# The projection behind the attention in pairs of column groups, three of its eight pairs of K tiles by seven products

## The chip, the cores and the metric

The kernel runs on one core of a Trainium2 chip. The metric is device time in microseconds (us) of the whole program, the median of several executions. Within the core TensorE (PE) multiplies, VectorE (DVE) and ScalarE (ACT) prepare operands and evict results, SyncE (SP) and GpSimd (POOL) issue the transfers from memory. Each engine works through its own queue in order; semaphores release an instruction that waits for another engine.

## The reference

One layer of a streaming encoder on 256 tokens (T) of width 2048 (D), float32 throughout. The parts that the change touches are the output projection of the cross attention and the start of the second feed-forward:

```python
x = x + 0.5 * swiglu(rms_norm(x, ffn1_norm[l]), ffn1_w_up[l], ffn1_w_down[l])
...                                   # in-projections, HGRN2, RG-LRU, gated merge
x = x + merged @ w_out[l]
x = x + cross_attention(rms_norm(x, xattn_norm[l]), rms_norm(mem, mem_norm[l]),
                        xattn_wq[l], xattn_wkv[l], xattn_wo[l])
x = x + 0.5 * swiglu(rms_norm(x, ffn2_norm[l]), ffn2_w_up[l], ffn2_w_down[l])
return rms_norm(x, final_norm)

def swiglu(h, w_up, w_down):          # D_FF = 5632
    gate, up = jnp.split(h @ w_up, 2, axis=-1)
    return (jax.nn.silu(gate) * up) @ w_down

def cross_attention(h, m, wq, wkv, wo):   # 4 heads of 512, 256 memory tokens
    ...
    o = jnp.einsum('bhsm,bmhd->bshd', p, v).reshape(B, S, D)
    return o @ wo
```

## The kernel before

**Split operands.** Every float32 operand is held as two parts: a high part `h` (ACT's copy into the matmul type, L153) and a low part `l` (DVE's difference between the value and `h`, L154). A product is three matmuls: high by high, low by high and high by low. `xh`, `xl` are the parts of activations, `h`, `l` those of weights; `h` and `l` come from pools of three buffers each, and a weight buffer `raw` of 1 MB from a pool of three (in the second feed-forward two more, `raw2`, in memory that earlier stages use for other tiles). PSUM has eight banks (`acc`).

**Pairs of K tiles.** In the feed-forwards and in the projection `out` behind the gated merge, two K tiles are multiplied with two groups of columns at a time. A *mixed* (plain) pair does this by eight products, 24 matmuls. A *fast* pair does it by seven products, 21 matmuls, in the manner of Strassen and Winograd: it needs sums and differences of the operands (`xs`, a difference for part of them `xd`; L601) and three differences of the weights (`td`, L334, L336, L338), which are split too (their high part by ACT, their low part `tl` by DVE, both as two pieces of 1024 columns). In an *added* pair (M) the low part of the weights costs DVE nothing: ACT writes the negative copy and an accumulating transfer issued by POOL adds the float32 weights to it. Of the first four groups of the second feed-forward 25 fast pairs are *ready*: their `td` was worked out during the middle of the program, went to memory as a tensor `t`, and is loaded (1024 KB) beside the rest of the weights (768 KB).

**Stages.** Projections of the memory to keys and values; first feed-forward; the in-projections, the two recurrences and their merge; `out`; the projection for q, beside which the heads of the attention run as generators that are advanced a step at a time (`pump`); `o`, the projection behind the attention; the second feed-forward in eleven groups of eight pairs; the final norm. `out` takes its products from a table of pairs, `"m0 f1 M2 f3 m4 f5 M6 m7"`, once for each two column groups (`pair_products`), and `add_residual` adds a finished pair of column groups to the residual stream: six operations of DVE and a copy of ACT once the early banks are done, five at the end.

**`o` before.** It multiplies by `rows_product` (L388): 16 blocks of four K tiles by 512 columns, 24 matmuls each (L393, L394, L399), in the order of `OUT_ORDER`. For each block the weights of 1 MB are split whole (`h` by ACT, `l` 128x2048 by DVE). A finished column group c is added to the residual by `to_residual` (two operations, L1297), and `to_ffn(c)` makes operands of the second feed-forward from it: eight transposes by TensorE (L550), scaled copies, `xh`, `xl`, then eight sums of 128x128 (L601) and their parts. For c = 0 to 2 this stands in `o`, for c = 3 it comes in two halves within the first pairs of the feed-forward.

**The second feed-forward before.** Its first group (`ffn_order`) has fast pairs 0 to 5, all ready, and mixed pairs 6 and 7; in the second group pairs come as 1, 3, 4, 0, 2, 5, 6, 7. Weights are asked for up to two pairs ahead. The order within each engine's queue comes from the tile framework's scheduler, in which loads may move far ahead of the place where the code names them.

## Time and profile before

| | |
|---|---|
| median of 3 runs | 2406.14 us (2405.97 to 2406.42) |
| profiled execution | 2406.76 us |
| its span, first to last instruction | 2405.0 us |
| granted TensorE clock | 0.999 |
| PE, DVE, ACT busy | 2393.3, 2054.2, 1560.6 us |
| transfers | 640 MB, 266 GB/s mean |

A row of the chain of waits gives start, length, engine, tile, line and how many instructions were joined; a row of the windows gives the stretch, its length, and busy time and instructions of PE, PEld (weight loads), DVE, ACT, POOL, then the granted clock, the DMA share and GB/s; a row of a timeline gives start, length, engine, line, operation, what is written from what, shapes and count, and in brackets how long the engine was idle before and what ended it. The projection `o` ends at 1721.93 us; `out` runs from 1430 to 1516.

### The profile page before, as it was taken

To read this page: it belongs to the slowest core of one execution; us is meant where nothing else is said; L and a number is where in the kernel's file an instruction comes from. 1 tells how busy PE (TensorE), PEld (TensorE's weight loads), DVE (VectorE), ACT (ScalarE), POOL (GpSimd) and SP (SyncE) were. 2 spreads that over 40 slices of the span, in tenths; PEclk is the share of its full clock that TensorE was granted. 3 is DMA by queue.
4 is the path that set the end of the run, shared out by engine and by line. 5 is a ranking of instruction groups with operands and counts; after the bars stand their busy time and mean duration, and the time that the engine had idled before them with its cause. 6 is when DMAs were issued, how large, how long until landed. Compare 5 with 4: busy or idle time off the path is not lost.

```text
span 2405.0 us, 31008 instructions
## 1 busy us (share of the span) xinstructions
PE 2393.3 (100%) x12053; PEld 1991.5 (83%) x12053; DVE 2054.2 (85%) x2335; ACT 1560.6 (65%) x1594; POOL 120.1 (5%) x174
## 2 busy tenths in 40 slices
PE   9999999999999999999999999999999999999998
PEld 7888888888888888888888888888888888888887
DVE  7679999999999866778678788765799999999995
ACT  6756777777777654454576456655676677777774
POOL 0000000000000000000000000000000000000000
PEclk9999999999999999999999999999999999999999
DMA  8876889999999757767678768764687899999993
GB/s 301 309 254 223 268 266 266 273 274 278 276 276 276 266 216 291 265 243 289 258 276 334 281 243 262 294 223 162 215 321 299 317 276 276 274 274 273 274 272 129
DMA packets 98739, 640.03 MB, mean 266 GB/s; under 512 B 10976, under 2 KB 11488, under 8 KB 32928
## 3 DMA queue, kind: packets, MB, share of 16 engines
q1 hardware_dynamic: 74160, 493.61, 54.8%
q0 software_dynamic: 24288, 144.19, 24.5%
q8 instruction: 94, 1.54, 0.2%
q14 instruction: 53, 0.43, 0.0%
q10 hardware_dynamic: 144, 0.26, 0.0%
HBM read 601.18 MB, written 36.83 MB: 265 GB/s over the span
## 4 chain that ended last, share of the span: by engine, by line
PE 97%; DVE 2%; DMA 1%; ACT 0%; issue 0%; SPq 0%; ACTq 0%; DVEq 0%
PE acc L698 38%; PE acc L700 19%; PE acc L367 11%; PE acc L393 7%; PE acc L394 7%; PE acc L399 7%; PE acc L370 6%; PE acc L738 1%; PE acc L550 1%; DVE tl L154 1%; DVE l L154 0%; PE acc L1342 0%; PE acc L1088 0%; DMA raw<-t 0%; PE acc L1367 0%
## 5 line engine op out<-in xcount | busy, mean ns | idle before, releaser
L153 ACT ACTIVATE h<-raw 128x2048 fp32r<-128x2048 f32 (+3 forms) x420 | 683.2, 1640 | 412.6 <-PE acc L394 135.0
L154 DVE TENSOR_TENSOR l<-raw,h 128x2048 fp32r<-128x2048 f32 (+2 forms) x365 | 751.6, 2060 | 227.4 <-ACT h L153 224.9
L698 PE MATMUL acc<-h,xh 128*128 128x512 f32 x1221 | 474.6, 391 | 0.6 <-ACT h L153 0.5
L698 PE MATMUL acc<-h,xl 128*128 128x512 f32 x1221 | 473.1, 390 | 0.0
L153 ACT ACTIVATE h<-td 128x1024 fp32r<-128x1024 f32 x287 | 301.0, 1055 | 172.3 <-DVE td L334 53.7
L154 DVE TENSOR_TENSOR tl<-td,h 128x1024 fp32r<-128x1024 f32 x287 | 348.9, 1220 | 13.7 <-ACT h L153 11.8
L698 PE MATMUL acc<-h,hidop 128*128 128x512 f32 x1408 | 351.4, 391 | 0.0
L698 PEld LDWEIGHTS acc<-h,hidop 128*128 128x128 f32 x1408 | 262.7, 188 | 53.8
L698 PEld LDWEIGHTS acc<-h,xh 128*128 128x128 f32 x1221 | 229.1, 188 | 54.6 <-ACT h L153 5.8
L698 PEld LDWEIGHTS acc<-h,xl 128*128 128x128 f32 x1221 | 229.3, 188 | 46.7
L393 PE MATMUL acc<-h,ops 128*128 128x512 f32 x576 | 226.1, 393 | 0.0
L394 PE MATMUL acc<-h,ops 128*128 128x512 f32 x576 | 224.4, 390 | 0.0
L367 PE MATMUL acc<-ops,h 128*128 128x512 f32 x896 | 217.7, 393 | 0.0
L700 PE MATMUL acc<-tl,xh 128*128 128x512 f32 x660 | 193.0, 394 | 0.3 <-DVE tl L154 0.3
L367 PEld LDWEIGHTS acc<-ops,h 128*128 128x128 f32 x896 | 164.1, 188 | 32.6
L700 PE MATMUL acc<-l,hidop 128*128 128x512 f32 x704 | 190.7, 389 | 0.0
L334 DVE TENSOR_TENSOR td<-raw 128x1024 f32<-128x1024 f32 x146 | 178.0, 1219 | 3.5 <-DMA raw<-wout 2.3
L700 PE MATMUL acc<-l,xh 128*128 128x512 f32 x561 | 156.7, 390 | 0.0
L700 PEld LDWEIGHTS acc<-l,hidop 128*128 128x128 f32 x704 | 132.1, 188 | 27.8
L700 PEld LDWEIGHTS acc<-tl,xh 128*128 128x128 f32 x660 | 120.7, 188 | 33.8 <-DVE tl L154 10.1
L399 PE MATMUL acc<-l,ops 128*128 128x512 f32 x576 | 142.3, 389 | 0.0
L399 PEld LDWEIGHTS acc<-l,ops 128*128 128x128 f32 x576 | 108.1, 188 | 22.4
(270 smaller groups left out, 3014.4 us busy)
## 6 DMA issues: line engine op xcount, KB each, us to landing
raw<-wu SPq DMA_DIRECT2D x151, 1024.0 KB, 6.9
raw<-wd SPq DMA_DIRECT2D x88, 1024.0 KB, 7.3
l<-wu POOLq DMA_DIRECT2D x59, 768.0 KB, 8.7
raw<-win SPq DMA_DIRECT2D x40, 1024.0 KB, 4.9
raw<-wg SPq DMA_DIRECT2D x32, 1024.0 KB, 5.4
prep<-wu POOLq DMA_DIRECT2D x25, 1024.0 KB, 7.1
t<-prep POOLq DMA_DIRECT2D x25, 1024.0 KB, 4.6
raw<-t SPq DMA_DIRECT2D x25, 1024.0 KB, 6.5
```

The source lines that it names most:

```text
L153: done["high"] = act.activation(h, raw, ACT.Copy).ins
L154: done["low"] = dve.tensor_tensor(out=l, in0=raw, in1=h.bitcast(F32), op=ALU.subtract).ins
L334: dve.tensor_tensor(out=two[0], in0=raw[:, None, :512].broadcast_to([P, 2, 512]), in1=two[1], op=ALU.subtract)
L367: pe.matmul(acc, h[:, k * P:(k + 1) * P], xs[k], start=k == 0, stop=False)
L370: done["product"] = pe.matmul(acc[:, :T], l[:, k * P:(k + 1) * P], xs[k][:, :T], start=False, stop=k == KT - 1).ins
L393: pe.matmul(accs[t], x[:, t * P:][:, :P], h[j], start=first and j == 0, stop=False)
L394: pe.matmul(accs[t], x[:, T + t * P:][:, :P], h[j], start=False, stop=False)
L399: done["product"] = pe.matmul(accs[t], x[:, t * P:][:, :P], l[j], start=False, stop=last and j == 3).ins
L550: pe.transpose(acc[:, z * T + t * P:][:, :P], tile[:, t * 512 + (2 * y + z) * P:][:, :P], ident)
L698: pe.matmul(acc, a, b, start=start, stop=False)
L700: done["product"] = pe.matmul(acc, ah, bl, start=False, stop=stop).ins
L738: pe.transpose(acc[:, z * T + t * P:][:, :P], hid[t][:, (2 * y + z) * P:][:, :P], ident)
```

## The change

`o` is computed like `out`: by `pair_products` with the same table, in two rounds of two column groups, each with eight pairs of K tiles, three of them by seven products (f1, f3, f5), two added (M2, M6), three plain. The weights `wo` are laid out for pairs. The heads write their results into operands for pairs, with the sums that fast pairs need. `add_residual` takes the place of `to_residual`. The operands of the second feed-forward come in halves of four transposes for every c: those of c = 0 and 1 behind pairs 1, 3, 5 and 6 of the second round of `o`, those of c = 2 and 3 within the first pairs of the feed-forward. The first group of the feed-forward now has mixed pairs 0 and 7 and fast pairs 1 to 6, pair 0 added; still 25 pairs are ready. The heads are advanced by four steps instead of two within the projection for q, and have more, smaller steps.

```diff
@@ -22,9 +22,6 @@
 HEADS = 4
 HD = D // HEADS
 LEVELS = [1, 2, 4, 8, 16, 32, 64]
-
-OUT_ORDER = [(g, kq) for g in range(2) for kq in range(3)] + [(0, 3), (1, 3)]
-OUT_ORDER += [(g, kq) for g in (2, 3) for kq in range(4)]
 BACC = {"dynamic_dma_scratch_size": 1024}
@@ -47,7 +44,7 @@
 KINDS = {"m": "mixed", "M": "mixed", "f": "fast", "a": "fast"}
-PAIRED = {"out": "m0 f1 M2 f3 m4 f5 M6 m7"}
+PAIRED = {"out": "m0 f1 M2 f3 m4 f5 M6 m7", "o": "m0 f1 M2 f3 m4 f5 M6 m7"}
 def kinds(name):
@@ -65,7 +62,7 @@
-    out = [("mixed" if p > 5 else "fast", 0, p) for p in range(8)] if every else first(0)
+    out = [("fast" if 0 < p < 7 else "mixed", 0, p) for p in range(8)] if every else first(0)
     down = [("down", 0, 1, c, 0) for c in range(4)]
     for g in range(1, NG):
         if every:
@@ -165,6 +162,8 @@
             src = wd[e[4], e[3]] if e[0] == "down" else wu[e[1], e[2]]
             kind = "fast" if e[0] == "fast" else "plain"
             if name == "ffn1" and e[0] == "mixed" and f"M{e[2]}" in FIRST[e[1]]:
+                kind = "added"
+            if name == "ffn2" and e == ("mixed", 0, 0):
                 kind = "added"
             if e[0] == "down" and e[4] < NG - 1 and e[4] % 2 == 0 and e[3] % 2 and (e[4] or name == "ffn1"):
                 kind = "added"
@@ -209,8 +208,7 @@
             plan_rows(name, w, g)
     plan_pairs("out", wout)
     plan_columns("q", wq, range(KT))
-    for g, kq in OUT_ORDER:
-        plan.append((("o", g, kq), wo[g, kq], "plain"))
+    plan_pairs("o", wo)
     first_second = len(plan)
     plan_ffn("ffn2", wu2, wd2)
@@ -579,8 +577,8 @@
             h, l = slot(F32R, "xh"), slot(F32R, "xl")
             split(h[:, :512], l[:, :512], g)
             less = None
-            if every and q == 3:
-                if not i:
+            if every and 2 * q + i in (0, 7):
+                if not q:
                     xd.append(slot(F32R, "xd"))
                 less = [xd[-1][:, a:a + 256] for a in (512 * i, 512 * i + 256)]
             if not every and 2 * q + i in BOTH:
@@ -1291,10 +1289,6 @@
             merge(g // 2, accs)
             accs = []
-    def to_residual(c, accs):
-        for t in range(2):
-            o = xt[c][:, t * 512:(t + 1) * 512]
-            dve.tensor_tensor(out=o, in0=accs[t], in1=o, op=ALU.add)
     while under_way:
         next(under_way.pop(0)[1])
     parts.close()
@@ -1317,8 +1311,9 @@
     while under_way:
         next(under_way.pop(0)[1])
     parts.close()
-    parts.enter_context(scope(prep=2, kt=2))
+    parts.enter_context(scope(wide=3, kt=2))
     qs, os = Operands(), Operands()
+    pairs_o = Pairs("o", os)
     rmem = scoped["norms"].tile([P, T], F32, name="rmem", tag="rstd")
     nc.gpsimd.dma_start(rmem, kept_r)
@@ -1366,10 +1361,12 @@
                 s, p = vs[t], ps[:, t * 512:(t + 1) * 512]
                 pe.matmul(acc, s[:, j * P:(j + 1) * P], p, start=(t == 0), stop=False)
                 pe.matmul(acc[:, :T], s[:, 512 + j * P:512 + (j + 1) * P], p[:, :T], start=False, stop=(t == 1))
-            os.add(summed(acc))
-            if j == 1:
-                yield
-        yield True
+            if j % 2 == 0:
+                x = pairs_o.room()
+            os.add(summed(acc, out=x[:, j % 2 * T:][:, :T]))
+            if j % 2:
+                pairs_o.add()
+            yield j == 3
     for m in range(KT):
         if m % 4 == 2:
@@ -1382,43 +1379,40 @@
         qs.add(summed(acc))
         if m % 4 == 3:
             side.append(head_at)
-        pump(2)
+        pump(4)
     pairs2, sums2, sq4 = [], [], TokenSquares()
     def gain2(k):
         return col("ffn2_norm", k)
-    def to_ffn(c):
-        out = []
-        sums2.append(operand_pairs(turned(xt[c]), gain2, c, slot(name="xg"), out, every=True))
-        pairs2.extend(out)
-        if c < 2:
-            sums2.pop(0)()
-
-    out3 = []
-
-    def to_ffn_half(y):
+    halves = {}
+
+    def to_ffn(c, y):
         if not y:
-            out3.append(slot(name="xg"))
-            out3.append([])
-        sums = operand_pairs(turned(xt[3], [y]), gain2, 3, *out3, every=True)
-        pairs2.append(out3[1][-1])
-        if y:
+            halves[c] = slot(name="xg"), []
+        sums = operand_pairs(turned(xt[c], [y]), gain2, c, *halves[c], every=True)
+        pairs2.append(halves[c][1][-1])
+        if y and c < 2:
+            sums()
+        elif y and c == 2:
+            sums2.append(sums)
+        elif y:
             sums2.extend(lambda n=n: sums(((0, n), (1, n))) for n in ("less", "sums"))
-    accs = {}
-    for c, kq in OUT_ORDER:
-        if kq == 0:
-            accs[c] = [bank(), bank()]
-        while len(os.tiles) < 4 * kq + 4:
+    def before_o(g, p):
+        while len(os.tiles) < 2 * p + 2:
             pump(2)
-        rows_product(accs[c], os.tiles, weights("o", c, kq), 4 * kq, kq == 0, kq == 3)
-        flush(late)
+
+    def behind_o(g, p):
         pump(2)
-        if kq == 3:
-            to_residual(c, accs[c])
+        if g and p in (1, 3, 5, 6):
+            flush(late, 1)
+
+    for g in range(2):
+        pair_products("o", g, pairs_o, add_residual, behind_o, before_o)
+        for c in (2 * g, 2 * g + 1):
             sq4.add(c)
-            late += [lambda c=c: to_ffn(c)] if c < 3 else [lambda y=y: to_ffn_half(y) for y in range(2)]
+            late += [lambda c=c, y=y: to_ffn(c, y) for y in range(2)]
     middle.close()
     assert not made_ahead and not under_way
@@ -1553,7 +1547,7 @@
         "wu1": up(a["ffn1_w_up"][0]), "wd1": down(a["ffn1_w_down"][0]),
         "win": win, "wv": rows(w[:, 2048:3072]), "wg": wg, "wab": wab, "wout": pairs(a["w_out"][0]),
         "wq": columns(a["xattn_wq"][0]), "wk": columns(wkv[:, :D]), "wvm": in_quarters(rows(wkv[:, D:])),
-        "wo": rows(a["xattn_wo"][0]),
+        "wo": pairs(a["xattn_wo"][0]),
         "wu2": up(a["ffn2_w_up"][0]), "wd2": down(a["ffn2_w_down"][0]),
     }
```

Line numbers after the change are two or three lower than before (L154 is L151, L698 is L696, L700 is L698, L601 is L599).

On DVE, around the end of `o` (the residual additions of column group 3 and what follows them), before; `l` and `tl` are low parts of weights, `xl` of activations, `x3_94` a residual tile, the numbers behind the names those of buffers in order of their allocation:

```order
L154 TENSOR_TENSOR tl_14126<-raw_14119,h_14125 128x1024 x2
L1297 TENSOR_TENSOR x3_94<-acc_14002,x3_94 128x512
L1297 TENSOR_TENSOR x3_94<-acc_14003,x3_94 128x512
L154 TENSOR_TENSOR l_14181<-raw_14176,h_14180 128x1536
L520 TENSOR_REDUCE stdt_14445<-sst_13472 128x2
L154 TENSOR_TENSOR tl_14185<-raw2_14178,h_14184 128x1024 x2
L154 TENSOR_TENSOR l_14249<-raw2_14244,h_14248 128x1536
```

and with the change, from the first of the five final additions of the second round (`x2_93` and `x3_94`):

```order
L686 TENSOR_TENSOR x2_93<-acc_13889,x2_93 128x512
L151 TENSOR_TENSOR xl_14136<-xs_14185,xh_14135 128x512
L151 TENSOR_TENSOR xl_14182<-xs_14185,xh_14181 128x512
L686 TENSOR_TENSOR x2_93<-acc_13890,x2_93 128x512
L686 TENSOR_TENSOR x3_94<-acc_13892,x3_94 128x512
L686 TENSOR_TENSOR x3_94<-acc_13891,x3_94 128x512 x2
L151 TENSOR_TENSOR l_14311<-raw2_14306,h_14310 128x1536
L151 TENSOR_TENSOR tl_14261<-raw2_14254,h_14260 128x1024 x2
```

Five additions and two low parts of c = 1's sums stand where two additions stood, and the next low part is that of the third pair (`l_14311`, `raw2`), ahead of the second pair's `tl_14261`.

On DVE, towards the end of the feed-forward's first group, before (`l_14419` and `l_14455` are the mixed pairs 6 and 7, `xs_14369` the sums of c = 3):

```order
L154 TENSOR_TENSOR l_14387<-raw_14382,h_14386 128x1536
L154 TENSOR_TENSOR xl_14240<-xs_14369,xh_14239 128x512
L601 TENSOR_TENSOR xs_14369<-xg_14231,xs_14369 128x128
L154 TENSOR_TENSOR tl_14391<-raw_14384,h_14390 128x1024 x2
L154 TENSOR_TENSOR xl_14287<-xs_14369,xh_14286 128x512
L154 TENSOR_TENSOR l_14419<-raw_14417,h_14418 128x2048
L523 RECIPROCAL rtok_14446<-stdt_14445 128x2
L154 TENSOR_TENSOR l_14455<-raw2_14453,h_14454 128x2048
```

and with the change (`l_14506` and `tl_14510` are pair 6, now fast, `l_14551` is pair 7, `xs_14536` the sums of c = 3):

```order
L151 TENSOR_TENSOR l_14506<-raw_14501,h_14505 128x1536
L151 TENSOR_TENSOR xd_13955<-xs_14496,xd_13955 128x256
L151 TENSOR_TENSOR tl_14510<-raw2_14503,h_14509 128x1024 x2
L599 TENSOR_TENSOR xs_14536<-xg_14403 128x128 x2
L599 TENSOR_TENSOR xs_14536<-xs_14536,xg_14403 128x128
L599 TENSOR_TENSOR xs_14536<-xg_14403 128x128
L599 TENSOR_TENSOR xs_14536<-xg_14403,xs_14536 128x128
L599 TENSOR_TENSOR xs_14536<-xs_14536,xg_14403 128x128
L599 TENSOR_TENSOR xs_14536<-xg_14403 128x128
L599 TENSOR_TENSOR xs_14536<-xg_14403,xs_14536 128x128
L151 TENSOR_TENSOR l_14551<-raw2_14549,h_14550 128x2048
```

The eight sums of c = 3 stand behind pair 6's low parts now, and one plain pair follows them instead of two.

On SP, where two loads of the first group's ready pairs were issued before, among the weights for q (`t0_1` holds the differences of pair 1):

```order
L307 DMA raw_12506<-wq 128x2048
L307 DMA raw_12512<-wq 128x2048
L325 DMA raw2_14178<-t0_1_96 128x2048
L323 DMA raw2_14244<-wu2 128x1536
L307 DMA raw_12558<-wq 128x2048
```

and with the change, at the end of the weights for `o`:

```order
L305 DMA raw_14144<-wo 128x2048
L321 DMA raw_14252<-wu2 128x1536
L323 DMA raw_14308<-t0_2_96 128x2048
L321 DMA raw_14355<-wu2 128x1536
L323 DMA raw2_14254<-t0_1_95 128x2048
L321 DMA raw2_14306<-wu2 128x1536
L323 DMA raw_14357<-t0_3_97 128x2048
```

The two loads into `raw2` have moved from the projection for q to behind the last weights of `o`; the memory of `raw2` holds the eviction buffer `ev` of `o` until then.

## The prediction

> **What bounds the kernel now.** I read the page's busy shares first, then the chain of waits, then windows over the stages that the change touches, and last VectorE's timeline there.
>
> ```profile
> PE 2393.3 (100%) x12053; PEld 1991.5 (83%) x12053; DVE 2054.2 (85%) x2335; ACT 1560.6 (65%) x1594; POOL 120.1 (5%) x174
> ...
> PE 97%; DVE 2%; DMA 1%; ACT 0%; issue 0%; SPq 0%; ACTq 0%; DVEq 0%
> ```
>
> TensorE is busy the whole span and carries 97% of the chain. So matmuls that are taken away shorten the run, as long as nothing else comes too late for the ones that stay. The windows say where something might (the columns are length, then busy time and instructions of PE, PEld, DVE, ACT and POOL, granted clock, DMA share, GB/s): the first row is the stage `out`, the next two are `o`, the last three the start of the second feed-forward.
>
> ```profile
> 1430.00:1510.00 80.00, 80.00 (x364) 66.01 (x363) 69.57 (x74) 53.88 (x53) 5.35 (x8) 1.00 0.86 270
> 1627.00:1670.00 43.00, 43.00 (x198) 35.42 (x197) 22.68 (x30) 18.99 (x23) 0.00 (x0) 1.00 0.46 158
> 1670.00:1722.00 52.00, 52.00 (x244) 43.27 (x243) 36.09 (x53) 32.20 (x47) 0.00 (x0) 1.00 0.49 175
> ...
> 1735.00:1765.00 30.00, 30.00 (x134) 24.86 (x133) 27.78 (x37) 22.71 (x24) 0.00 (x0) 1.00 0.89 325
> ```
> ```profile
> 1722.00:1797.00 75.00, 74.94 (x338) 61.65 (x337) 70.95 (x77) 58.98 (x63) 0.00 (x0) 1.00 0.85 312
> 1797.00:1850.00 53.00, 52.94 (x238) 43.54 (x237) 52.04 (x49) 35.80 (x33) 0.00 (x0) 1.00 0.84 316
> ```
>
> TensorE never pauses in `o`, where VectorE is idle for 36.2 of 95 us (22.68 and 36.09 busy). Behind it VectorE is idle for only 4.05 of 75 us, then 0.96 of 53: it just keeps up. That is the tight place of this change.
>
> **The change, part by part.** The chain gives TensorE's pace (start, length, what, how many). T0 is where `o` ends: 1721.93.
>
> ```profile
> 1675.70 0.87 PE acc L550 x8
> ```
> ```profile
> 1721.93 3.17 PE acc L698 x14
> 1725.10 1.59 PE acc L700 x7
> 1726.69 0.44 PE acc L550 x4
> ...
> 1751.46 3.63 PE acc L698 x16
> 1755.09 1.81 PE acc L700 x8
> ...
> 1760.53 1.81 PE acc L700 x8
> ...
> 1776.32 8.05 DMA raw<-t
> ...
> 1848.12 1.07 ACT h L153
> 1849.24 1.20 PE acc L698 x4
> ```
>
> *Products.* A pair of eight products is 24 matmuls and takes 3.63 + 1.81 = 5.44 us, one of seven is 21 and takes 3.17 + 1.59 = 4.76: 0.68 less, or 0.227 us a matmul. `o` had 16 blocks of 24 matmuls. It now has 2 x 8 pairs, six of them by seven products: 6 x 0.68 = -4.08 us. The first group of the second feed-forward has two pairs of eight before and after, so nothing there.
>
> The Trainium skill ("TensorE: Matmul & The Clock Gate", section "Back-to-back issue gap") gives about 131 ns for a matmul of 512 columns in a sustained stream; the 18 matmuls would then be worth 2.4 us, and the sum below would end at about 2408.0. The rows above speak against it for this kernel.
>
> *Transposes.* The three blocks of eight (0.87) and two of four (0.44) become eight of four: 3.5 us in both. But the one for c = 2 moves behind T0, with c = 3's halves: T0 comes 4.08 + 0.87 = 4.95 us earlier, and the first group is 0.88 us longer.
>
> *VectorE in `o`.* Prices come from its timeline, start to start (first rows: beginning of the second feed-forward; last: stage `out`).
>
> ```profile
> 1721.74 1.29 DVE L1297 TENSOR_TENSOR x<-acc,x 128x512 f32<-128x512 f32 x2 [2.79 <-PE acc L399]
> 1722.95 1.75 DVE L154 TENSOR_TENSOR l<-raw,h 128x1536 fp32r<-128x1536 f32 x1
> ...
> 1727.25 1.76 DVE L154 TENSOR_TENSOR l<-raw,h 128x1536 fp32r<-128x1536 f32 x1
> 1728.93 0.69 DVE L154 TENSOR_TENSOR xl<-xg,xh 128x512 fp32r<-128x512 f32 x1
> 1729.66 2.36 DVE L154 TENSOR_TENSOR tl<-raw,h 128x1024 fp32r<-128x1024 f32 x2
> 1731.98 1.76 DVE L154 TENSOR_TENSOR l<-raw,h 128x1536 fp32r<-128x1536 f32 x1
> ```
> ```profile
> 1742.65 0.29 DVE L601 TENSOR_TENSOR xs<-xg 128x128 f32<-128x128 f32 x1
> 1742.85 0.29 DVE L601 TENSOR_TENSOR xs<-xg,xs 128x128 f32<-128x128 f32 x1
> ...
> 1749.01 2.29 DVE L154 TENSOR_TENSOR l<-raw,h 128x2048 fp32r<-128x2048 f32 x1
> 1751.21 0.17 DVE L523 RECIPROCAL rtok<-stdt 128x2 f32<-128x2 f32 x1
> ...
> 1753.69 0.69 DVE L781 TENSOR_TENSOR ev<-acc,ev 128x512 f32<-128x512 f32 x1
> ...
> 1761.02 0.69 DVE L789 TENSOR_TENSOR ev<-acc,ev 128x512 f32<-128x512 f32 x1 [2.11 <-PE acc L700]
> ```
> ```profile
> 1464.58 2.29 DVE L154 TENSOR_TENSOR l<-raw,h 128x2048 fp32r<-128x2048 f32 x1 [1.92 <-ACT h L153]
> ...
> 1470.99 1.23 DVE L334 TENSOR_TENSOR td<-raw 128x1024 f32<-128x1024 f32 x1 [0.52 <-DMA raw<-wout]
> 1472.25 0.69 DVE L336 TENSOR_TENSOR td<-raw,td 128x512 f32<-128x512 f32 x1
> 1472.98 0.69 DVE L338 TENSOR_TENSOR td<-raw,td 128x512 f32<-128x512 f32 x1
> 1473.59 1.28 DVE L688 TENSOR_TENSOR x<-acc,x 128x512 f32<-128x512 f32 x2
> ```
>
> That makes 1.66 for `l` of 1536 columns, 2.3 for both `tl`, 2.2 for `l` of 2048, 0.60 for an operation of 128x512, 0.20 for one of 128x128, and 2.4 for the three that make `td` (1.2, 0.6, 0.6). Six pairs of seven cost 6 x (2.4 + 1.66 + 2.3) = 38.2, six m pairs 6 x 2.2 = 13.2, the M pairs nothing, and this replaces 16 x 2.2 = 35.2. Two evictions of eleven operations (13.2) replace four of two (4.8). The preparation of c = 2, 4.0 (four low parts, eight sums), leaves. Together +20.6 us against 36.2 idle. Stage `out` has the same table of pairs and the same evictions, and there TensorE is busy 80.00 of 80.00 with VectorE at 69.57; I take no stall in `o`, and keep one as a rival.
>
> *VectorE behind T0.* Before, from 1721.74 to 1753.69, 32.0 us, it did all that the first group needs. Now it has two more final adds (1.2), the two low parts of c = 1's sums (1.2) and all of c = 2 (4.0); of c = 3 one difference is gone (two of 0.20 and a low part of 256 columns, estimated 0.34 between 0.20 and 0.60: -0.74). The pairs' own low parts come out equal: pair 0 needs none, but before that pair was ready by T0. Sum +5.7. Besides, in its queue the `l` of pair 2 stands next after the final adds, and it needs ACT's `h`, which needs pair 0's buffer: that is free 3.63 us after T0, and the copy takes 1.4 by this row:
>
> ```profile
> 1736.03 1.48 ACT L153 ACTIVATE h<-raw 128x1536 fp32r<-128x1536 f32 x1
> ```
>
> VectorE ends the adds at about T0 + 3.0 and waits until 5.2: 2.2 us. So it is late by 5.7 + 2.2 = 7.9 us against T0. What absorbs this? The last low part (pair 7's) was ready at 1753.69 and used at 1760.53, 6.8 us of slack, and TensorE gets 0.88 us more to do: 7.7. So TensorE waits little up to there, but VectorE enters the next groups with no lead, and there it has only its idle time, at most 4.05 + 0.96 = 5.0 us up to 1850, where TensorE already waits for it (ACT's `h`, late behind `tl`, ends the wait at 1849.2). Bounds for the whole: with every idle microsecond used, -4.95 + 7.9 - 5.0 = -2.1 us; with none, +2.9. I walked through the queues in the new order by these prices: TensorE waits 1.2 us at pairs 6 and 7 of the first group (the sums of c = 3's last half and pair 7's `l` come late; products of 7 are mixed into 6 already), 1.25 at the first pair of the second group (two `tl` stand ahead of the gate's additions, which free the banks), 0.1, then 0.9 at the turn to the `hidop` products and 0.8 at its seventh pair. That is 4.25 us, between the bounds and nearer the lower one, because the idle 2.11 at 1761 was a wait for TensorE and goes, while the one behind the 8.05 us transfer stays.
>
> *ScalarE* stays under 80% of every window above, and one copy per eviction (0.6) is new. *SP's queue:* two loads for ready pairs stood among those for q, 210 us ahead of T0:
>
> ```profile
> 1512.04 0.33 SPq L325 DMA_DIRECT2D raw<-t  x1
> 1512.47 0.38 SPq L323 DMA_DIRECT2D raw<-wu  x1
> ```
>
> Now they stand at the end of `o`, behind an add that frees `ev`, and the load of pair 3's differences is queued behind them. By my walk that add ends about 7 us ahead of T0 (the early part of the eviction follows the sixth pair, so two pairs and two transposes, 11.7 us, ahead of T0; ACT's copy and six additions of 0.60 follow), and the loads land about T0 and T0 + 3, just in time.
>
> **Sum.** The profiled execution took 2406.76 us (span 2405.0 and 1.76 around it), 0.62 above the median of the runs. -4.08 + 4.25 = +0.2: 2406.9 profiled, **2406.3** beside the median.
>
> **Rivals.**
>
> *VectorE hides it all.* For it: `out` runs so without a pause, and a scheduled queue may take the idle time better than my walk. Against it: the +7.9 us against 5.0. Then 2406.14 - 4.08 = 2402.1.
>
> By the Trainium skill ("Perfetto Trace Analysis", section "Identifying the Most-Contended Engine") the weight loads' share, not that of matmuls, tells how near TensorE is to its limit: 83% here, less than VectorE's 85%. By that rule this rival would lose its chance, while the chain of waits, 97% TensorE, leaves it some.
>
> *The ready pairs' transfers become the bound (slower).* Each needs 768 and 1024 KB, 1.835 MB; at the 325 GB/s of 1735 to 1765 that takes 5.65 us, against 4.76 of TensorE. Before, one pair's worth was loaded at 1512. Without that head start five ready pairs run behind by 0.89 each: 4.4 us, 2410.7. It decides if loads take 8 us (as the 8.05 above) rather than the median here:
>
> ```profile
> raw<-t SPq DMA_DIRECT2D x25, 1024.0 KB, 6.5
> ```
>
> Against it: the loads of `o` itself leave the DMA at a share of 0.46 to 0.49, so raw buffers can fill before T0.
>
> *VectorE already fails in `o`'s second half.* There it has 3 x 6.36 + 3 x 2.2 + 6.6 (an eviction) + 8.0 (c = 0 and 1) + 1.7 (a first `l` for the feed-forward) = 42.0 us of work in 5 x 5.44 + 3 x 4.76 + 1.75 = 43.2. One wait like the 1.92 in `out` takes the margin away: about 2.4 us more with two of them, 2408.7. It decides if the `td` operations queue behind an eviction.
>
> **How the numbers follow.** Forecast 0.60 (2404.1 to 2409.1, its bounds less 0.62), hidden 0.20, transfers 0.12, `o` 0.08. The range 2402.0 to 2409.6 takes in the first and last, most of the second, and leaves the transfers out. About 0.2%, 4.8 us, is what can be told from no change here. Even the whole gain of 4.08 stays below that, so faster by more gets 0.05 (T0 earlier than I think); slower by more, above 2411, 0.11, the transfers and what I overlook; 0.84 for within.
>
> **What would show it.** Right: in the changed profile T0 is 4 to 5 us earlier with TensorE busy all through `o`; then TensorE is idle some 4 us between T0 and T0 + 130, ended by DVE `l`, `tl` or `xl` or ACT's `h` behind them; VectorE has no idle time but some 2 us just behind T0. Wrong: idle TensorE ended by DMA `raw<-t` (transfers); idle TensorE inside `o`; or none at all, with the end 4 us earlier (hidden). If T0 is earlier by much less than 4 us, the pace of 0.227 us or the transposes are misjudged.

## The result

| | median, us | lowest to highest | executions |
|---|---|---|---|
| before | 2405.5 | 2404.6 to 2407.5 | 12 |
| changed | 2410.8 | 2409.8 to 2413.2 | 12 |

The changed kernel takes 1.0023 times as long, 95% interval 1.0014 to 1.0032: 5.3 us more (3.4 to 7.7). The forecast was 2406.3, its range ended at 2409.6. So this is slower, by a little more than can be told from no change.

The changed kernel's page and its windows, from the start of the projection for q to the second group of the feed-forward (columns as before):

```profile
PE 2392.0 (99%) x12035; PEld 1988.5 (83%) x12035; DVE 2082.9 (86%) x2399; ACT 1581.2 (66%) x1621; POOL 124.6 (5%) x179
...
PE 91%; DVE 5%; DMA 2%; issue 1%; ACT 1%; SPq 0%; ACTq 0%; DVEq 0%
```
```profile
1510.00:1600.00 90.00, 88.21 (x504) 76.30 (x503) 67.87 (x117) 55.22 (x94) 4.29 (x8) 1.00 0.60 216
1600.00:1660.00 60.00, 59.02 (x305) 49.65 (x304) 47.72 (x85) 37.51 (x58) 3.90 (x6) 1.00 0.64 197
1660.00:1713.00 53.00, 53.00 (x241) 43.85 (x241) 41.93 (x51) 38.48 (x43) 2.60 (x3) 1.00 0.81 247
1713.00:1766.00 53.00, 49.57 (x220) 39.91 (x219) 47.12 (x73) 40.06 (x56) 0.00 (x0) 0.97 0.81 299
1766.00:1820.00 54.00, 54.00 (x242) 44.13 (x241) 53.60 (x53) 40.79 (x38) 0.00 (x0) 1.00 0.82 302
```

18 matmuls are gone, but TensorE, which hardly paused here before, stands idle in three of these five stretches, and in one of them its granted clock is below 1. TensorE's table of waits, for the whole program, names what ended them (line, releaser, us in all, times, longest):

```profile
PE acc L698 <- DVE tl L151: 2.9, 2, 2.6
PE acc L548 <- DVE x L686: 1.7, 2, 1.4
...
PE acc L1337 <- ACT ops L432: 1.0, 1, 1.0
...
PE acc L698 <- DVE l L151: 0.8, 1, 0.8
```

Counted in the trace from one matmul's start to the next against its pace, TensorE loses 2.4 us at 1517 to 1523 (the transposes that open the projection for q), 1.1 at 1630 (the last head's scores, beside the start of `o`), 4.8 at 1728 to 1735 (the second pair of the feed-forward) and 1.0 at 1760 (its pairs 6 and 7). That is 9.3 us in one execution against 4.08 saved. From the first product of `out` to the end the two profiled executions differ by 5.05 us (975.09 before, 980.14 changed), near the 5.3 of the medians; the spans differ by less (3.7), because the changed execution happened to reach `out` 1.4 us earlier. Each kernel below reaches it between 1428.3 and 1431.0, so this says nothing of the change.

**The third place**, the dearest. VectorE's, then ScalarE's, then SP's timeline of the changed kernel:

```profile
1721.89 2.60 DVE L686 TENSOR_TENSOR x<-acc,x 128x512 f32<-128x512 f32 x4
1728.72 1.76 DVE L151 TENSOR_TENSOR l<-raw,h 128x1536 fp32r<-128x1536 f32 x1 [4.23 <-ACT h L150]
1730.40 2.35 DVE L151 TENSOR_TENSOR tl<-raw,h 128x1024 fp32r<-128x1024 f32 x2
```
```profile
1724.08 1.06 ACT L150 ACTIVATE h<-raw 128x1024 fp32r<-128x1024 f32 x1 [2.55 <-DMA raw<-t]
...
1725.66 1.05 ACT L150 ACTIVATE h<-raw 128x1024 fp32r<-128x1024 f32 x1
...
1727.22 1.47 ACT L150 ACTIVATE h<-raw 128x1536 fp32r<-128x1536 f32 x1
```
```profile
1715.75 0.33 SPq L323 DMA_DIRECT2D raw<-t  x1
1716.31 0.33 SPq L321 DMA_DIRECT2D raw<-wu  x1
```

The two loads that stood at 1512 before are issued at 1715.75 and 1716.31, 3.4 us ahead of the end of `o` (1719.10). The differences of pair 1 land at 1723.99. ScalarE waits 2.55 us for them, with pair 2's `h` queued behind; VectorE waits 4.23 us for that `h`, with pair 1's `tl` queued behind; TensorE waits for the `tl`. One late load stops three queues in turn. And the wait costs more than its length:

```profile
1728.00:1731.00 3.00, 1.03 (x5) 0.53 (x3) 2.28 (x2) 2.97 (x7) 0.00 (x0) 1.00 0.00 0
1731.00:1735.00 4.00, 3.33 (x9) 2.38 (x10) 4.00 (x5) 3.14 (x4) 0.00 (x0) 0.59 0.80 264
```

After 2.64 us without work TensorE is granted a clock of 0.59 on average over the next 4 us, and matmuls then start some 0.58 us apart instead of 0.23.

Two things stand behind this. The first is the order in VectorE's queue. The high parts of pair 1's differences were ready at 1725.14 and 1726.71, and `tl` takes 1.2 us for each. In front of pair 2's `l` it would have ended at about 1728 (an estimate from these rows), 1 us before TensorE stopped at 1729.03 (its next start, 1731.67, less the 2.64). The second is what held the load back, in ScalarE's and VectorE's timelines:

```profile
1707.84 1.92 ACT L150 ACTIVATE h<-raw 128x2048 fp32r<-128x2048 f32 x1 [1.89 <-DMA raw<-wo]
```
```profile
1709.79 2.29 DVE L151 TENSOR_TENSOR l<-raw,h 128x2048 fp32r<-128x2048 f32 x1 [3.11 <-ACT h L150]
1712.00 0.68 DVE L680 TENSOR_TENSOR ev<-acc,ev 128x512 f32<-128x512 f32 x1
```

The last weights of `o` are issued at 1697.72 and take 10.03 us. ScalarE waits for them and VectorE for ScalarE, and the early additions of the eviction, which free `ev`, stand in VectorE's queue behind the `l` of these weights. They begin at 1712.00, 4.7 us after TensorE's last product of the sixth pair, and end at 1715.7.

**The first place** lies 200 us ahead of all that the prediction looked at. From POOL's timeline the loads of the keys and values, of the changed kernel and then of the one before, and below them the weight load of `out` that VectorE waits for next, from the chain of the changed kernel (7.39 us) and from the list of DMA issues of before (4.8 us):

```profile
1469.43 1.08 POOL L1324 DMA_DIRECT2D kt<-k  x2 [10.22 <-DMA t<-prep]
1490.25 1.44 POOL L1327 DMA_DIRECT2D vs<-v  x2
```
```profile
1504.59 1.13 POOL L1329 DMA_DIRECT2D kt<-k  x2 [12.64 <-PE acc L700]
1505.69 1.08 POOL L1332 DMA_DIRECT2D vs<-v  x2
```
```profile
1483.88 7.39 DMA raw<-wout
```
```profile
raw<-wout SPq DMA_DIRECT2D x1, 1024.0 KB, 4.8
```

The first head's keys and values are loaded up to 35 us earlier, beside the last weights of `out`. From that load the chain runs through VectorE's queue to the final additions of `out`, for which the transposes at 1517 wait. What both places share is one line of the change that works out no number: the pools of the stage of q and `o` are three wide buffers and the keys instead of two others and the keys. With that the keys lie on memory that `out` leaves early, and the wide buffers on the memory of `raw2`.

### The profile page after: what moved, and what is told of

It reads as the page before. It is cut to its first block, busy times and chain, and to the rows that moved or that the text cites. A ratio compares the mean times of both kernels' runs of the same rounds, so it can differ in the third digit from the quotient of the medians.

```text
span 2408.7 us, 31068 instructions
## 1 busy us (share of the span) xinstructions
PE 2392.0 (99%) x12035; PEld 1988.5 (83%) x12035; DVE 2082.9 (86%) x2399; ACT 1581.2 (66%) x1621; POOL 124.6 (5%) x179
## 4 chain that ended last, share of the span: by engine, by line
PE 91%; DVE 5%; DMA 2%; issue 1%; ACT 1%; SPq 0%; ACTq 0%; DVEq 0%
PE acc L696 37%; PE acc L698 19%; PE acc L365 10%; PE acc L391 5%; PE acc L392 5%; PE acc L397 5%; PE acc L368 5%; DVE l L151 2%; DVE tl L151 1%; PE acc L736 1%; DMA raw<-wo 1%; ACT h L150 1%; DMA raw<-wout 1%; DVE td L332 0%; PE acc L548 0%
## 5 line engine op out<-in xcount | busy, mean ns | idle before, releaser
L150 ACT ACTIVATE h<-raw 128x2048 fp32r<-128x2048 f32 (+3 forms) x415 | 672.1, 1631 | 384.8 <-PE acc L392 100.3
L151 DVE TENSOR_TENSOR l<-raw,h 128x2048 fp32r<-128x2048 f32 (+2 forms) x360 | 735.7, 2044 | 209.8 <-ACT h L150 206.9
L696 PE MATMUL acc<-h,xh 128*128 128x512 f32 x1221 | 474.1, 392 | 0.6 <-ACT h L150 0.5
L696 PE MATMUL acc<-h,xl 128*128 128x512 f32 x1221 | 472.3, 390 | 0.0
L150 ACT ACTIVATE h<-td 128x1024 fp32r<-128x1024 f32 x299 | 313.1, 1055 | 176.5 <-DVE td L332 58.7
L151 DVE TENSOR_TENSOR tl<-td,h 128x1024 fp32r<-128x1024 f32 x299 | 362.6, 1217 | 12.5 <-ACT h L150 10.5
L696 PE MATMUL acc<-h,hidop 128*128 128x512 f32 x1408 | 352.4, 391 | 0.0
L696 PEld LDWEIGHTS acc<-h,hidop 128*128 128x128 f32 x1408 | 262.6, 188 | 54.1 <-ACT h L150 0.4
L696 PEld LDWEIGHTS acc<-h,xh 128*128 128x128 f32 x1221 | 229.3, 188 | 55.2 <-ACT h L150 5.9
L696 PEld LDWEIGHTS acc<-h,xl 128*128 128x128 f32 x1221 | 229.4, 188 | 46.3
L698 PE MATMUL acc<-tl,xh 128*128 128x512 f32 x660 | 196.8, 396 | 2.9 <-DVE tl L151 2.9
L332 DVE TENSOR_TENSOR td<-raw 128x1024 f32<-128x1024 f32 x152 | 184.8, 1216 | 14.1 <-DMA raw<-wo 7.9
L698 PE MATMUL acc<-l,hidop 128*128 128x512 f32 x704 | 190.4, 389 | 0.0
L391 PE MATMUL acc<-h,ops 128*128 128x512 f32 x448 | 175.9, 393 | 0.0
L392 PE MATMUL acc<-h,ops 128*128 128x512 f32 x448 | 174.5, 389 | 0.0
L698 PE MATMUL acc<-l,xh 128*128 128x512 f32 x561 | 157.7, 390 | 0.8 <-DVE l L151 0.8
L698 PEld LDWEIGHTS acc<-l,hidop 128*128 128x128 f32 x704 | 132.1, 188 | 27.7
L698 PEld LDWEIGHTS acc<-tl,xh 128*128 128x128 f32 x660 | 121.3, 188 | 36.7 <-DVE tl L151 12.9
L698 PEld LDWEIGHTS acc<-l,xh 128*128 128x128 f32 x561 | 105.2, 188 | 23.7 <-DVE l L151 1.2
L368 PEld LDWEIGHTS acc<-ops,l 128*128 128x128 f32 x896 | 115.4, 191 | 4.7
```

What stands on the lines that cost most here:

```text
L150: done["high"] = act.activation(h, raw, ACT.Copy).ins
L151: done["low"] = dve.tensor_tensor(out=l, in0=raw, in1=h.bitcast(F32), op=ALU.subtract).ins
L332: dve.tensor_tensor(out=two[0], in0=raw[:, None, :512].broadcast_to([P, 2, 512]), in1=two[1], op=ALU.subtract)
L368: done["product"] = pe.matmul(acc[:, :T], l[:, k * P:(k + 1) * P], xs[k][:, :T], start=False, stop=k == KT - 1).ins
L391: pe.matmul(accs[t], x[:, t * P:][:, :P], h[j], start=first and j == 0, stop=False)
L392: pe.matmul(accs[t], x[:, T + t * P:][:, :P], h[j], start=False, stop=False)
```

## The experiments

Each was timed against the kernel before, 11 executions of its own (7 for one of them). "Lost" is TensorE's time counted as above, in the profiled execution: at the start of q (A), at the last head (B), at the second pair of the feed-forward (C), at its pairs 6 and 7 (D) and behind (E). The next two columns are the time from the first product of `out` to that of the feed-forward (T0), and from there to the end. The ratio is to the kernel before on the same chip. There its median lay between 2405.4 and 2406.4 us, so medians of runs on different chips differ by some tenths for that alone. The columns from A on are those of one execution.

| kernel | median, us | ratio to before, 95% | A | B | C | D | E | `out` to T0 | T0 to end |
|---|---|---|---|---|---|---|---|---|---|
| before | 2405.5 | | 0 | 0 | 0 | 0 | 0.4 | 291.9 | 683.2 |
| changed | 2410.8 | 1.0014 to 1.0032 | 2.4 | 1.1 | 4.8 | 1.0 | 0.5 | 290.6 | 689.6 |
| e1 keys back | 2409.6 | 1.0006 to 1.0024 | 0 | 0.9 | 2.5 | 1.8 | 0.9 | 288.0 | 689.3 |
| e2 turn of buffers | 2408.2 | 1.0000 to 1.0018 | 4.1 | 1.0 | 0 | 1.4 | 0.9 | 292.2 | 686.4 |
| e3 before, memory alone | 2412.0 | 1.0017 to 1.0039 | 1.9 | 0 | 4.1 | 0 | 0 | 293.8 | 686.8 |
| e4 both | 2406.0 | 0.9992 to 1.0010 | 0 | 0.7 | 0 | 0.8 | 0.6 | 287.7 | 684.9 |
| e8 both, again | 2405.8 | 0.9991 to 1.0009 | 0 | 0.8 | 0 | 1.4 | 1.0 | 287.8 | 686.0 |
| e5 both, all by eight | 2408.9 | 1.0004 to 1.0022 | 0 | 0 | 0 | 0.6 | 1.1 | 291.2 | 685.6 |
| e12 keys back, fast pairs later | 2406.2 | 0.9990 to 1.0008 | 0 | 0 | 0 | 1.9 | 1.5 | 287.5 | 688.2 |
| e13 e12, operands earlier | 2405.6 | 0.9991 to 1.0009 | 0 | 0 | 0 | 1.6 | 0.8 | 287.4 | 686.3 |

**The change of memory alone.** The kernel before, with this line and nothing else:

```diff
-    parts.enter_context(scope(prep=2, kt=2))
+    parts.enter_context(scope(wide=3, kt=2))
```

> The kernel before with one line changed: the pools of the stage of q and `o` are those of the changed kernel (three wide buffers, then the keys); products, orders and evictions are as before, and the wide buffers stand empty. Memory theory: the keys are loaded beside `out` and the two `raw2` loads at the end of `o`, so a wait of about 2.4 us turns up behind `out` and one behind the end of `o`; 2405.5 + 2.4 + 1 to 5 = 2409 to 2413. Rival (the loss comes from the added operations): no change, 2405.5.

2412.0, 6.6 us more than before, by allocating buffers that nothing uses. POOL's timeline, the waits and a window of this kernel:

```profile
1469.12 1.08 POOL L1329 DMA_DIRECT2D kt<-k  x2 [10.14 <-DMA t<-prep]
```
```profile
PE acc L698 <- ACT h L153: 3.0, 2, 2.5
PE acc L550 <- DVE x L688: 1.2, 2, 0.9
```
```profile
1732.00:1736.00 4.00, 3.51 (x10) 2.81 (x11) 4.00 (x9) 4.00 (x6) 0.00 (x0) 0.59 0.06 20
```

Both waits of the changed kernel are here, at the same places, with the same fall of the clock, in a kernel without a single new operation. The loss comes from where the buffers lie. But the memory alone does not hold the `raw2` loads back: of what earlier stages keep there the keys are used last, and TensorE reads them for the last time at 1634. The loads are issued 90 us later, because the scheduler has put them behind pair 3's, which waits for an ordinary weight buffer (SP's timeline, `t` of pair 3 and then of pair 1, and 1.2 us later pair 2's `wu`):

```profile
1723.76 0.96 SPq L325 DMA_DIRECT2D raw<-t  x2
```

**Undoing it, half by half.** The keys' pool first, so that it lies where `out` still works:

```diff
-    parts.enter_context(scope(wide=3, kt=2))
+    parts.enter_context(scope(kt=2, wide=3))
```

> The changed kernel with the two pools of the stage of q and `o` laid out in the other order (keys first, then the wide buffers), so that the first head's keys lie where `out` still works, as they did before the change. Memory theory: in the changed kernel the first head's keys and values are loaded at 1469 to 1491, beside the last weights of `out` (7.39 us for one of them instead of 4.76), and the 2.5 us in which TensorE waits at 1517 to 1523 come from that; with the keys back behind `out` that wait is gone and the time falls by about 2.4 us, to about 2408.4. Rival (the wait comes from the order of VectorE's queue): the wait stays and the time is that of the changed kernel, 2410.8. Both: the waits at 1630 and 1728 to 1735 stay.

TensorE's idle time at the start of q is gone (first row), and the median falls by 1.2 us, half of what was expected; C and D together still cost 4.3. The time behind T0 hardly changed (689.3 against 689.6) although C is smaller, and why is not shown:

```profile
1510.00:1530.00 20.00, 20.00 (x113) 17.27 (x113) 15.32 (x26) 13.48 (x26) 0.00 (x0) 1.00 0.64 231
1728.00:1731.00 3.00, 1.49 (x6) 0.92 (x7) 3.00 (x4) 2.74 (x4) 0.00 (x0) 1.00 0.60 203
1731.00:1735.00 4.00, 4.00 (x21) 3.33 (x20) 4.00 (x4) 3.97 (x7) 0.00 (x0) 1.00 0.96 349
```

The last row is of use besides: after this kernel's pause, 1.8 us at the longest, the clock stays at 1.00; in the changed kernel, after 2.64, it fell.

The other half leaves the memory and lets other loads use it: the loads for pair 1's differences and pair 2's weights go to the ordinary weight buffers, those for pairs 2 and 3 to `raw2`.

```diff
-        if "raw2" in scoped and next(loads) % 5 > 2:
+        if "raw2" in scoped and next(loads2) % 5 > 2:    # loads2 = count(0)
```

> The changed kernel, in which only the turn between the two sorts of weight buffers of the second feed-forward is shifted by two loads: the differences of pair 1 and the weights of pair 2 go into the buffers that are free early, those of pairs 2 and 3 into the two whose memory `o` still holds. Memory theory: TensorE's wait of 2.64 us at 1729 and the 4 us at a granted clock of 0.59 behind it (together 4.9 us) come from loads that wait for `o`'s eviction buffer; they go, and the time falls by 4 to 5 us, to 2406 to 2407. Rival (VectorE has 5.7 us more work there, whatever is loaded when): some 1 to 2 us of waiting go and the rest turns up within the next 10 us, 2409 to 2410.

```profile
1728.00:1733.00 5.00, 5.00 (x26) 4.10 (x24) 4.88 (x5) 4.97 (x8) 0.00 (x0) 1.00 0.64 249
```

C is gone without a trace, nothing turned up in its place within 10 us, and the median fell by 2.6 us. That is less than the 4 to 5 expected. A is dearer here, 4.1 us, but in the profiled execution, the slowest of the eleven; whether that explains the median is not shown.

> The changed kernel with both edits: keys back behind `out`, and the turn of the weight buffers shifted. Memory theory: both gains add up, 2410.8 - 2.4 - 4.5 = about 2404, that is 1 to 2 us less than before the change; what then is left of the 4.08 us of matmuls saved is eaten by the waits of 1.25 us at 1630 and about 1 us at 1760. Rival (added work of VectorE): not below 2408.

> The kernel with both edits once more, on the same chip as the three others: 2404 to 2407 as in its first runs; the profile is to show which of its waits differ between executions.

Both together: 2406.0, and 2405.8 in a second set. That is 4.9 us below the changed kernel, more than the two gains one by one (3.8), and level with the kernel before. The expected 2404 was not reached in the median, though the profiled execution took 2403.9; the eleven lie from 2403.9 to 2408.1, a wider band than the kernel before has.

**What the products are worth.** As e4, with `"m0 m1 M2 m3 m4 m5 M6 m7"` for `o`, all pairs by eight.

> The kernel with both edits of memory (keys back behind `out`, turn of the weight buffers shifted), with the three fast pairs of `o` made plain pairs of eight products, so that nothing is left of the 18 matmuls saved, nor of the differences and early evictions. If the products are worth what the pace says, this costs 4.1 us: 2406.0 + 4.1 = about 2410, with no new wait. Rival (what the products save is lost again in `o` and behind it to VectorE's extra 20 us): 2405 to 2407, and TensorE's waits at 1628 and 1750 are gone in this kernel.

2408.9, 3.1 us above e8 on the same chip; 4.1 was expected. The time from `out` to T0 grows by 3.3 to 3.5, and B, 0.7 to 0.8, is missing in this kernel. So the pace of 0.227 us a matmul holds (18 of them are 4.08), and what the seven products cost in `o` itself is that one wait. It also shows that, with all 384 matmuls, the new arrangement is 2.8 us slower than the kernel before: behind T0, 685.6 against 683.2, of which 0.88 are the transposes that moved there.

**The beginning of the feed-forward.** As e4, with fast pairs 0 to 5 and plain pairs 6 and 7, as before the change.

> The kernel with both edits of memory, whose second feed-forward begins as before the change: fast pairs 0 to 5, plain pairs 6 and 7 (the number of products is the same). If the beginning with a pair of eight matters only for when what is loaded and prepared, as the memory theory has it, the first pair's differences (1 MB more to land ahead of the end of `o`, 3.9 us more of VectorE there) now come late and the time rises by 1 to 4 us, 2407 to 2410. Rival (the order of pairs is worth nothing once the buffers are right): 2406, and the waits of 0.8 us at 1750 go, since two plain pairs then follow the sums of c = 3.

2406.3 (0.9993 to 1.0011): no difference. In the profiled execution D shrinks to one wait of 0.4, but 1.4 us are lost at the first two pairs (1721 to 1735): there the order only chooses the place.

**Another plan of memory**: two wide buffers in `o`, and the two `raw2` above them.

> The changed kernel with another plan of memory: two wide buffers in `o` instead of three, and the two extra weight buffers of the second feed-forward above them, where only the keys lie, so that their loads need not wait for an eviction; the keys lie where `out` still works. Memory theory: no wait at 1517, none at the end of `o`; 2405 to 2406 as with both edits, or 1 us less, since the two loads come early as before the change. Rival (two wide buffers are too few: the low parts of one fast pair must be used up before the next pair's differences can be made): TensorE waits in `o`, 2408 or more.

2406.6 (0.9993 to 1.0011). C is gone here too, by the early loads themselves, but a wait of 1.85 us appears at 1650 in `o`. It is no better than e4.

**Less work for VectorE at the end of the group.** As e4, with pair 7 an added pair.

> The kernel with both edits of memory, and pair 7 of the second feed-forward's first group made an added pair as pair 0 is (its low part by ScalarE and an accumulating transfer, 2.2 us less for VectorE there). If the waits of 0.8, 0.4 and 0.2 us at 1751 to 1755 come from VectorE's 5.7 us of added work in that group (the last low parts late), they shrink to under 0.5 us in all and the time falls by about 1 us, to 2404.8. Rival (they come from ScalarE's copies, which get one more of 1.9 us): they stay or grow, 2406 or more.

2406.1 (0.9993 to 1.0010): no gain. D grew to 2.9 us in the profiled execution (the slowest of its eleven), ended by ScalarE, which waits 1.87 us for a load with one of its two new copies (1.90 us) behind it:

```profile
1751.86 2.00 ACT L150 ACTIVATE h<-raw 128x1024 fp32r<-128x1024 f32 x2 [1.87 <-DMA raw<-t]
1753.77 1.90 ACT L296 ACTIVATE h<-raw 128x2048 fp32r<-128x2048 f32 x1
```
```profile
1751.00:1754.00 3.00, 1.08 (x6) 0.58 (x4) 2.10 (x3) 2.14 (x3) 0.00 (x0) 1.00 0.82 263
1754.00:1758.00 4.00, 3.40 (x14) 2.50 (x15) 3.48 (x9) 3.98 (x5) 0.00 (x0) 1.00 1.08 284
```

In the windows of that place TensorE works for 1.08 us of 3, and the granted clock is 1.00 there and behind.

**The fast pairs of `o` later.** As e4, with `"m0 M1 f2 f3 m4 f5 M6 m7"`; e11 is this and e9's added pair in one kernel.

> The kernel with both edits of memory, with the fast pairs of `o` at places 2, 3 and 5 instead of 1, 3 and 5 and the added pairs at 1 and 6 instead of 2 and 6 (as many of each kind). If the wait of 0.7 to 1.1 us at 1628 (the last head's scores) comes from the first fast pair's differences, for which VectorE waits 4.2 us at 1614 with the last sums of q queued behind them, the wait goes and the time falls by 0.8 us, to 2405. Rival (VectorE is simply late there because the sums for pairs were added to the heads): the wait stays and the time is 2406; a new wait at 1640 to 1660, where two fast pairs now follow each other, would make it 2407 or more.

> Both edits of memory, pair 7 added and the fast pairs of `o` later, in one kernel: if the three causes are independent, 2406.0 - 1 - 0.8 = about 2404, 1.5 to 2 us less than before the change. If the waits are only passed on to the next place, 2405.5 to 2406.

2410.4 (1.0007 to 1.0024) and 2410.5 (1.0006 to 1.0024), 4.0 and 4.1 us above the kernel before on that chip, where e4 is 0.5 above it on its own chip. B is gone in e10, as expected of the first theory there, but C is back with 4.7 us. VectorE's timeline and a window of e10:

```profile
1718.51 3.20 DVE L686 TENSOR_TENSOR x<-acc,x 128x512 f32<-128x512 f32 x5
1726.01 1.76 DVE L151 TENSOR_TENSOR l<-raw,h 128x1536 fp32r<-128x1536 f32 x1 [4.30 <-ACT h L150]
```
```profile
1732.00:1735.00 3.00, 3.00 (x11) 2.33 (x10) 3.00 (x3) 1.91 (x4) 0.00 (x0) 0.64 0.96 365
```

In this kernel `raw2` becomes free earlier, and the scheduler puts its load, pair 2's differences, ahead of pair 1's on SP:

```
L323 DMA raw2_14308<-t0_2_96 128x2048
L323 DMA raw_14254<-t0_1_95 128x2048
L321 DMA raw_14306<-wu2 128x1536
```

Pair 1's differences land 3.6 us behind T0 (in e8 0.5 us ahead of it), and VectorE's queue again has pair 2's `l` ahead of pair 1's `tl`. If that is the cause, the same table with the turn of buffers as the change has it, which brings pair 1's load to the front, must be free of it:

> The kernel of the run with the fast pairs of `o` at places 2, 3 and 5 and the keys back behind `out`, but with the turn of the weight buffers as the change has it (so this is the changed kernel with the keys back and the other places of the fast pairs). In its queue the differences of pair 1 now stand ahead of those of pair 2, and VectorE makes the low part of pair 1's differences ahead of pair 2's. If the wait at 1729 in the run before came from pair 1's load standing behind pair 2's, it goes, and so does the one at 1628: 2405 or less, 1 us less than before the change. Rival (with the fast pairs later, VectorE itself is too late at the end of `o`): the wait of 2 us and the fall of the clock behind it stay, 2409 to 2410.

It is: 2406.2, with neither A, B nor C. Here pair 1's differences land 0.9 us behind T0 and its `tl` stands ahead of pair 2's `l`; both changed at once, so which of the two counts is not separated. So a fast table for `o` without any wait is possible, and T0 then comes 4.4 us earlier than before.

**Where the rest goes.** In e12 all that was saved ahead of T0 is lost behind it: 688.2 against 683.2. Two windows of e12, and the same two of e13, where the halves of c = 0 and 1 become operands behind pairs 1, 2, 3 and 4 instead of 1, 3, 5 and 6:

```profile
1672.00:1717.00 45.00, 45.00 (x207) 36.94 (x206) 37.72 (x52) 32.17 (x40) 1.73 (x2) 1.00 0.77 237
1717.00:1765.00 48.00, 46.62 (x210) 37.41 (x209) 46.10 (x68) 42.05 (x55) 0.00 (x0) 1.00 0.88 327
```
```profile
1672.00:1717.00 45.00, 45.00 (x206) 36.94 (x205) 40.05 (x60) 32.68 (x44) 1.74 (x2) 1.00 0.79 243
1717.00:1765.00 48.00, 46.75 (x212) 37.75 (x212) 43.63 (x61) 40.77 (x54) 0.00 (x0) 1.00 0.88 328
```

> The kernel of the run before (keys back, fast pairs of `o` at places 2, 3 and 5), with the halves of c = 0 and 1 turned into operands behind pairs 1, 2, 3 and 4 of the second round of `o` instead of 1, 3, 5 and 6. This moves 2.8 us of VectorE's work (two low parts and the eight sums of c = 1) from around the end of `o` to where VectorE is idle for 7.3 of 45 us, and nothing else. If the waits at 1751 to 1755 (1.9 us) and behind them (1 us) are VectorE's lateness, they fall to under 0.7 us in all and the time to about 2404, 2 us less than before the change. Rival (they are ScalarE's, or the order of the sums of c = 3 behind pair 6): they stay and the time is 2406.

> The same with the halves behind pairs 1, 2, 3 and 5: the two low parts of c = 1's sums come ahead of the end of `o`, the sums themselves stay near it. Half of the effect by VectorE's lateness: waits at 1751 to 1755 of 0.7 to 1.2 us, 2405. Rival: 2406.

The work did move (VectorE 37.72 to 40.05 ahead of T0, 46.10 to 43.63 behind), but D went only from 1.9 to 1.6 and the median from 0.2 us below the kernel before to 0.1 below it, no difference. e14 took 2407.6 (1.0001 to 1.0018), above both: from 1717 to 1765 VectorE has as little to do in it as in e13 (43.40), yet TensorE is busy for 45.60 of 48 only. So 2.5 us less of VectorE's work in the first group do not remove its waits. That they come from the amount of VectorE's work is not borne out. E fell from 1.5 to 0.8. What holds D is open: with 2 us taken from VectorE, ScalarE (40.77 of 48) and the transfers (0.88) are nearly as full, and e9 shows a load ending such a wait.

No version measured here beats the kernel before: the best, e8, e9, e12 and e13, lie 0.1 to 0.3 us below it on their chips, and their intervals reach to either side of it.

## Why the prediction was wrong

**What bounds the kernel, the products, the transposes: right.** TensorE sets the time. The pace priced the 18 matmuls at 4.08 us, and e5 bears this out (3.3 to 3.5 us from `out` to T0, where B had taken 0.7 to 0.8 of it). With nothing in the way (e12) T0 comes 4.4 us earlier, where 4.95 was said.

Two small terms are off by the prediction's own rows: the three operations for `td` take 2.6 us from start to start, not 2.4 (1.2 us more in six pairs), and two waits of 1.92 less a margin of 1.2 are 2.6, not 2.4. Neither changes the forecast.

**VectorE in `o`: nearly right.** "I take no stall in `o`" held in its second half. TensorE was busy 53.00 of 53.00 from 1660 to 1713 of the changed kernel, so the rival that VectorE fails there fell. The 1.1 us at 1630, B, was missed: VectorE waits 4.56 us for the load of the first fast pair, up to 1616, with the last sums of q queued behind, and e10 and e12 show that it goes when the first fast pair comes later.

**The step that failed is the one on SP's queue**: "By the walk they land about T0 and T0 + 3, just in time." The first landed 4.9 us after T0. The walk took the add that frees `ev` to end 7 us ahead of T0; it ended 3.4 us ahead of it, because it stood behind the last pair's `l`, for whose weights (10.03 us to land) no wait had been reckoned. The load itself took 8.24 us where the walk left it 7, so 3.6 of the 4.9 us are the add and 1.2 the load. By this VectorE's wait for pair 2's `h`, in the sum with 2.2 us and an end at T0 + 5.2, measured 4.23 and ended at T0 + 9.6, with pair 1's `tl` behind it. The sum had no wait of TensorE here; it cost 4.8 us in the profiled execution, and moving these loads to other buffers gave back 2.6 us in the median (e2).

The measured 2410.8 is next to the 2410.7 of the rival of late transfers, which was given 0.12. That is luck in part. It had loads of 8 us as the point from which it decides, and ScalarE's 2.55 us did end with `DMA raw<-t`. But it had five ready pairs falling behind by 0.89 us each for want of bandwidth, and measured is one late landing that stopped three queues once: 2.64 us of TensorE's waiting and 1.7 of clock. Nor would the sign it named have shown it, since the releaser of TensorE's own wait is `DVE tl`, the sign of the forecast.

**What was not looked at at all** is POOL's queue. Three wide buffers for two others was read as a line that frees or holds `raw2`; that the same line moves the keys' loads by 35 us into `out`, 200 us ahead of the part of the program being changed, was not asked. The prediction had no term for it, and A took 2.4 us (half of it in the medians of e1 against the changed kernel, 1.2 us).

**VectorE behind T0: the second step that failed.** In the changed kernel the wait forecast at pairs 6 and 7 was 1.2 us, and measured 1.0; but the 1.25, 0.1, 0.9 and 0.8 us in the second group did not appear (TensorE is busy 54.00 of 54.00 from 1766 to 1820, while VectorE works for 53.60 of it without being late). Nor did they where C, a pause in which VectorE catches up, is gone: from 1765 to 1850 TensorE is busy 85.00 of 85.00 us in e4 and e13, 84.84 in e12. So 3.05 of the 4.25 us were not there.

Where the memory is put right, the forecast of no change is what comes out: e4, e8, e12 and e13 at 2405.6 to 2406.2 against 2406.3 said. That is luck in part, for the losses that make it lie elsewhere: B in e4 and e8, and behind T0 1.7 to 5.0 us more than before (e4 1.7, e8 2.8, e13 3.1, e12 5.0, with the 0.88 of the transposes). What they come from is open; that they come from VectorE alone was the reason given, and e13 and e14 speak against it.

## What to carry to other kernels

A line that only sizes or orders pools is a change of schedule: ask for each buffer that moves which transfer waits for that memory now, and which one no longer has to wait, on every queue and as far back as the memory was last used. Then look where the scheduler puts these loads, for in e3 the memory was free 90 us before they were issued. Such moves at two places cost 6.6 us there, in a kernel whose operations were untouched. And where engines work through queues in order, a late load is paid by whatever is queued behind the first instruction that needs it, so what stands in front in that queue matters as much as when the load lands.

## What the runs showed of the hardware

A short pause of TensorE can cost well over its length. In the changed kernel, e3, e10 and e11 its longest pause at the start of the feed-forward was 1.9 to 2.6 us, and 2 to 4 us after that pause began its granted clock was down to a half. It stayed there for 3.4 us in all four: in windows of 1 us from 1731 to 1736 the changed kernel was granted 0.86, 0.50, 0.50, 0.50 and 0.94, which makes 1.7 us of clock lost, and the others come to the same sum. The pauses of 1.8 us in e1 and 1.9 us in e9 left no such mark. Length alone doesn't decide at this border, as e11's timeline and windows show:

```profile
1728.89 0.73 PE L698 MATMUL acc<-tl,xh 128*128 128x512 f32 x2 [1.86 <-DVE tl L151]
1730.02 0.77 PE L698 MATMUL acc<-tl,xh 128*128 128x512 f32 x2 [0.40 <-DVE tl L151]
```
```profile
1730.00:1732.00 2.00, 1.98 (x8) 1.75 (x9) 2.00 (x3) 1.80 (x2) 0.00 (x0) 0.64 0.82 309
1732.00:1734.00 2.00, 2.00 (x7) 1.52 (x6) 2.00 (x2) 1.15 (x3) 0.00 (x0) 0.51 1.12 415
```

Here 1.86 us and a second pause of 0.40 us behind two matmuls were enough. The Trainium skill ("TensorE: Matmul & The Clock Gate", section "What's actually happening") has TensorE fall to half its clock after an idle window of about 3.4 us, and return after some 3.4 us of work. The half agrees with these rows, and 3.4 us is how long the clock stayed down. But the fall came after shorter pauses than that, and in e3, where TensorE works again from 1732.49, the clock was back about 2.8 us later (1735 to 1736: 0.84). What else decides it was not tried.

A load of 1 MB in the changed kernel took 4.7 us with next to nothing beside it (issued at 1517.24), 7.39 us beside up to three others (1483.88) and 8.24 us beside two to four (1715.75). That spread was part of both late landings.
